# Moving twelve column groups of a modulation product from the conformer stage into the front of the mixer stage

## The chip, the cores and the metric

The kernel runs on one core of a Trainium2 chip. The metric is the device time of one execution in microseconds; the time of the kernel before is the median of three runs. One further execution was profiled, and all rows below come from it.

## The reference, cut to what matters

All work is in float32 on 512 tokens of width 1024. Two attention layers come first (not touched by the change), then two layers of a second kind. Layer 0 mixes with a recurrence and long convolutions, layer 1 with a convolution module (the conformer); each is followed by a mixture of 16 experts. Every layer takes six modulation vectors from a small product of a conditioning vector with a large matrix:

```python
def _adaln(cvec, w_mod, b_mod, n_chunks):
    m = silu(cvec) @ w_mod[:, :n_chunks * D_MODEL] + b_mod[:n_chunks * D_MODEL]
    return [m[:, None, j * D_MODEL:(j + 1) * D_MODEL] for j in range(n_chunks)]

for l in range(2):
    sh1, sc1, g1, sh2, sc2, g2 = _adaln(c, w_mod[l], b_mod[l], 6)
    hl = modulate(rmsnorm(xl, norm1_g[l]), sh1, sc1)
    yl = even_mixer(hl) if l == 0 else conformer(hl)
    xl = xl + g1 * yl
    xl = xl + g2 * moe(modulate(rmsnorm(xl, norm2_g[l]), sh2, sc2))
xl = rmsnorm(xl, final_g)

def even_mixer(h):
    proj = h @ w_in                        # 1024 -> 2560 columns, ten groups of 256
    ...                                    # recurrence (RG-LRU), two FFT convolutions (Hyena)
    return concat([y_a, z]) @ w_out        # 1024 -> 1024
```

The change concerns `sh2, sc2, g2` of layer 1, that is `silu(c) @ w_mod[1][:, 3072:6144]`: a 1024 x 3072 matrix of 12.6 MB. Nothing reads them before the second mixture of experts.

## The kernel before, in words

The program is one long list per engine, made by a scheduler that keeps the order of the source where priorities say nothing else. The stages of the second block follow each other: `even_norm` and the ten projection groups of `even_mixer`, then `hyena` (FFT convolutions, with the out-projection among them), the routing, `moe(0)`, `conformer`, `moe(1)` and the last norm.

**The weight ring.** `wload` (L119 to L139) brings weights in tiles of 512 KB, two to a projection group, by DMAs that SyncE issues in order (L134). The tiles lie in a pool with the tag `ring`; `RE = (3, 3)` gives the mixer three such tiles and three pairs of split tiles, the conformer has rings (6, 4). `split` (L141 to L156) makes of each half tile a rounded copy `wh` on ScalarE (L153) and the rest `wl` on GpSimd (L154), and `mm3` (L158 to L161) multiplies the three pairs that matter. A projection group (`proj_feat`, L368 to L391) is 8 x 2 x 3 = 48 such matmuls of 512 columns, and its last line (L391) calls `fill(1)`.

**The filler.** `fill` (L171) runs one step of a generator `self.filler`, if there is one, and gives its instructions the priority of the place, so that they may stand between the next group's instructions. The generator `adaln` (L195 to L227) makes the modulation vectors: per step it loads two tiles of `w_mod` (1 MB), multiplies them in eight matmuls of 32 x 256 outputs in 32-column strips (L209; each is two records in the profile), and adds the product into `adr` on VectorE (L212 the first time, L214 after that). After the twelfth step, four small matmuls (L219) and one add (L222) put the result into `self.m2[1]`. `cvec` (L178 to L193) loads the conditioning vector and makes its silu. The conformer sets up this filler for column groups 12 to 23 (L1590 and L1591); its eight projection groups call `fill(1)` once by L391 and, from the fourth on, once more by L1636.

**The mixer.** `even_mixer` (L1326) calls `even_norm` and then ten groups of `w_in_2`, called W0 to W9 below. W0 to W3 feed the recurrence, W4 to W9 the convolutions; with W4 to W9 go the steps of the recurrence `rglru` (L1230 to L1247), whose matmuls write `z`, and the transposes `t` (L1362) of the convolved channels `cv`. The tables of the Fourier transform are loaded by `tables` (L1087, tile `dw`), issued from ScalarE's queue, and stand in ScalarE's list among the casts of L153.

## Time and profile before

| what | us |
|---|---|
| median of three runs (lowest to highest) | 3083.48 (3079.88 to 3089.67) |
| the profiled execution, its own time | 3082.83 |
| its span in the trace | 3080.8 |
| two attention layers | 0 to 1560 |
| norm and the ten groups of the mixer | 1560 to 1721 |
| hyena, out-projection, routing | 1721 to 1845 |
| first mixture of experts | 1845 to 2345 |
| conformer | 2345 to 2570 |
| second mixture of experts, last norm | 2570 to 3080 |

The stage limits are round numbers where the work changes; stages overlap at their edges. TensorE is busy for 90% of the span, and the mean clock granted to it is 0.952 of full speed. In the two mixtures of experts the DMA engines are busy nearly throughout; in the stages that the change touches they are not.

A row of a stretch gives, for each engine, its busy microseconds and in brackets the number of instructions, then the granted clock, the mean share in which the 16 DMA engines were busy, and GB/s. A row of a timeline gives start, length, engine, line, operation, output and inputs, count, and in square brackets the idle time before it and what ended it. A row of a chain gives start, length and what was running.

### The profile page before, as it was taken

What the parts mean: (1) busy time and instruction counts of PE and PEld (TensorE: products, weight loads), DVE (VectorE), ACT (ScalarE), POOL (GpSimd) and SP (SyncE); (2) the same over time, 40 slices, a digit from 0 to 9 for tenths busy, and PEclk for the clock granted to TensorE, in tenths of its full rate; (3) what the DMA queues carried; (4) which work ended last, traced back from release to release, by engine and by line L of the source; (5) the groups of instructions that cost most, each with busy time, mean ns of one, the idle gap of its engine ahead of it and who ended that gap; (6) DMA issues with size and microseconds to landing.
All of it is one profiled execution on the core that took longest, in us unless ns stands there. A gap on an engine that the chain in (4) does not pass through costs nothing.

```text
span 3080.8 us, 36122 instructions
## 1 busy us (share of the span) xinstructions
PE 2760.5 (90%) x14014; PEld 1717.2 (56%) x14014; DVE 1514.0 (49%) x2793; ACT 923.3 (30%) x1651; POOL 815.7 (26%) x689
## 2 busy tenths in 40 slices
PE   6889899999899999999998877998888997998887
PEld 2486567776588666765676764433333665333332
DVE  5886664656625645786356773222124663221222
ACT  3434343443423453434335321101002232110101
POOL 2243233332333334343534660000001431000000
PEclk8999899999899999999999888999999998999999
DMA  9632024222253214421331338999996574999996
GB/s 285 210 124 62 22 87 133 90 73 66 73 164 120 76 54 145 137 89 55 116 97 58 103 116 345 420 421 420 421 420 244 154 271 192 420 420 420 420 421 273
DMA packets 225306, 634.26 MB, mean 206 GB/s; under 512 B 12559, under 2 KB 141591, under 8 KB 175728
## 3 DMA queue, kind: packets, MB, share of 16 engines
q1 hardware_dynamic: 213344, 597.62, 51.7%
q0 software_dynamic: 7312, 25.96, 2.5%
q10 hardware_dynamic: 4480, 8.39, 0.7%
q8 instruction: 110, 1.80, 0.3%
q14 instruction: 60, 0.49, 0.1%
HBM read 612.87 MB, written 19.14 MB: 205 GB/s over the span
## 4 chain that ended last, share of the span: by engine, by line
PE 28%; DMA 19%; DVE 5%; POOL 2%; ACT 2%; issue 1%; SPq 0%; DVEq 0%; ACTq 0%; POOLq 0%
DMA mr<-in_exp_w_dram 10%; PE b L1859 10%; DMA mq<-in_exp_w_dram 8%; PE b L159 4%; PE b L161 4%; PE b L160 3%; PE av L763 1%; PE b L209 1%; PE b L1844 1%; PE q L275 1%; DVE lh L1262 0%; PE s L757 0%; DMA scratch<-sb 0%; PE b L324 0%; DVE f L1473 0%
## 5 line engine op out<-in xcount | busy, mean ns | idle before, releaser
L154 POOL TENSOR_TENSOR wl<-ring,wh 128x512 fp32r<-128x512 f32 x304 | 417.3, 1377 | 676.1 <-ACT wh L153 658.0
L153 ACT CAST wh<-ring 128x512 fp32r<-128x512 f32 x304 | 187.4, 620 | 505.9 <-PE b L161 366.6
L1859 PE MATMUL b<-mr,xs 128*64 128x512 f32 x1216 | 283.7, 617 | 37.2 <-DMA mr<-in_exp_w_dram 28.7
L159 PE MATMUL b<-hh,wh 128*128 128x512 f32 (+1 forms) x800 | 294.9, 369 | 3.0 <-DVE sc L621 3.0
L160 PE MATMUL b<-hh,wl 128*128 128x512 f32 (+1 forms) x800 | 290.6, 363 | 1.3 <-POOL wl L154 1.3
L161 PE MATMUL b<-hl,wh 128*128 128x512 f32 (+1 forms) x800 | 289.4, 363 | 0.1
L1859 PE MATMUL b<-mq,xs 128*64 128x512 f32 x832 | 189.2, 604 | 25.2 <-DMA mq<-in_exp_w_dram 16.8
L1859 PEld LDWEIGHTS b<-mr,xs 128*64 128x64 f32 x1216 | 90.1, 141 | 216.6 <-issue 154.6
L1801 POOL DMA_INDIRECT xg<-scratch,ix x16 | 15.5, 967 | 728.0 <-DVE ix L1795 687.5
L763 PE MATMUL av<-P,kv 128*64 128x512 f32 (+2 forms) x672 | 191.8, 518 | 3.0 <-ACT P L813 1.8
L1859 PE MATMUL b<-mr,sb 128*64 128x512 f32 x704 | 159.4, 597 | 18.5 <-DMA mr<-in_exp_w_dram 18.3
L159 PEld LDWEIGHTS b<-hh,wh 128*128 128x128 f32 x800 | 153.3, 192 | 32.4 <-issue 5.6
L160 PEld LDWEIGHTS b<-hh,wl 128*128 128x128 f32 x800 | 153.2, 192 | 26.9 <-issue 4.3
L161 PEld LDWEIGHTS b<-hl,wh 128*128 128x128 f32 x800 | 152.6, 191 | 25.0 <-issue 4.5
L362 PE MATMUL b<-wh,hh 128*128 128x256 f32 x512 | 148.9, 291 | 2.1 <-DVE kb L1160 1.3
L813 ACT ACTIVATE P<-s 128x512 f32<-128x512 f32 (+2 forms) x224 | 116.7, 551 | 113.8 <-PE s L760 110.0
L363 PE MATMUL b<-wl,hh 128*128 128x256 f32 x512 | 148.3, 290 | 0.3 <-POOL wl L154 0.3
L364 PE MATMUL b<-wh,hl 128*128 128x256 f32 x512 | 147.8, 289 | 0.4 <-DVE hl L345 0.4
L1883 DVE TENSOR_TENSOR yl<-yl,b 128x512 f32<-128x512 f32 x32 | 22.0, 688 | 254.1 <-PE b L1859 254.1
L1859 PEld LDWEIGHTS b<-mq,xs 128*64 128x64 f32 x832 | 60.2, 138 | 146.2 <-issue 101.6
L776 POOL TENSOR_TENSOR acc<-acc,P 128x256 f32<-128x256 f32 (+2 forms) x96 | 99.5, 1039 | 118.2 <-ACT P L813 94.2
L757 PE MATMUL s<-q1l,k 128*128 128x512 f32 (+2 forms) x288 | 113.2, 403 | 2.1 <-DVE sc L802 1.6
(564 smaller groups left out, 5681.4 us busy)
## 6 DMA issues: line engine op xcount, KB each, us to landing
mr<-in_exp_w_dram SPq DMA_DIRECT2D x120, 2048.0 KB
mq<-in_exp_w_dram SPq DMA_DIRECT2D x72, 2048.0 KB
ring<-in_w_mod_dram SPq DMA_DIRECT2D x96, 512.0 KB
ring<-in_w_in_dram SPq DMA_DIRECT2D x96, 512.0 KB
ring<-in_ada_w_dram SPq DMA_DIRECT2D x48, 512.0 KB
ring<-in_w_out_dram SPq DMA_DIRECT2D x32, 512.0 KB
bias<-in_BS_dram POOLq DMA_DIRECT2D x16, 512.0 KB, 3.8
bias<-in_BT_dram POOLq DMA_DIRECT2D x16, 512.0 KB, 4.0
```

The costliest lines, as they stand in the source:

```text
L153: nc.scalar.copy(h, src)
L154: nc.gpsimd.tensor_tensor(l, src, h.bitcast(F32), op=ALU.subtract)
L159: m(out, w[0], x[0], start=start, stop=False, skip_group_check=chk)
L160: m(out, w[1], x[0], start=False, stop=False, skip_group_check=chk)
L161: m(out, w[0], x[1], start=False, stop=stop, skip_group_check=chk)
L362: m(o, hh, wh[:, kk, :], start=(k == 0 and i % 2 == 0), stop=False, skip_group_check=True)
L363: m(o, hh, wl[:, kk, :], start=False, stop=False, skip_group_check=True)
L364: m(o, hl, wh[:, kk, :], start=False, stop=stop, skip_group_check=True)
L757: mm(ps, k1[i][:, kt * 128:kt * 128 + 128], q1[i][:, a:b], start=True, stop=False)
L763: mm(av[64 * i:64 * i + 64, a:b], vf(i, kt), P, start=start, stop=stop)
L813: nc.scalar.activation(p[:, :w], ps[:, :w], AF.Exp)
L1859: mm(ps[hf][64 * e:64 * e + 64, :], lhs(k, e), wt[:, e, k2, hf * 512:hf * 512 + 512], start=k == 0, stop=k == 7)
```

## The change

`even_mixer` now makes `cv2` and the filler for column groups 12 to 23 ahead of `even_norm`, takes two steps at once, one more after each of its ten groups by the old last line of `proj_feat`, and empties what is left after the last group. The conformer no longer does either, and its calls of `fill` have nothing to do.

```diff
@@ even_mixer
                 self.hh, self.hl = [self.chunks(hp, nm, KD, N, F32R) for nm in ("hh", "hl")]
+                z2 = self.cvec(tmp, "cv2")
+                self.filler = self.adaln(z2, A["w_mod"][1], 6 * D, self.v("b_mod1"), self.m2[1], tmp, (12, 24))
+                self.fill(2)
                 self.even_norm(tmp)
...
                     next(lru, None)
+                while self.filler is not None:
+                    self.fill(1)
             ub = [self.chunks(up, f"ub{p}", 4, N, F32R) for p in "hl"]
@@ conformer
-                z2 = self.cvec(tmp, "cv2")
-                self.filler = self.adaln(z2, A["w_mod"][1], 6 * D, self.v("b_mod1"), self.m2[1], tmp, (12, 24))
                 w1 = A["cf_w1"]
...
                     self.proj_feat([(wv, 8)], lambda k, s: (hh[k][:], hl[k][:]), (N,), ev)
-                    if c > 2:
-                        self.fill(1)
```

The steps are called M0 to M11 below. Three places show what the change does to the lists.

SyncE at the loads of the second and third projection group, before: only `w_in` tiles, two to a group.

```order
L134 DMA ring_14063<-in_w_in_dram 128x4x256
L134 DMA ring_14065<-in_w_in_dram 128x4x256
L134 DMA ring_14145<-in_w_in_dram 128x4x256
L134 DMA ring_14147<-in_w_in_dram 128x4x256
L134 DMA ring_14227<-in_w_in_dram 128x4x256
```

The same place after, with what each load waits for: `PE` is TensorE's last reading of the tile's old contents, `Pool` is GpSimd's last subtract from it, `DMAHW` an earlier load.

```order
L134 DMA ring_14036<-in_w_in_dram 128x4x256 [waits DMAHW0_49,Pool_49]
L134 DMA ring_14038<-in_w_in_dram 128x4x256 [waits DMAHW4_49,DMAHW3_49,Pool_49]
L134 DMA ring_14112<-in_w_mod_dram 128x4x256 [waits DMAHW5_49,DMAHW1_49,PE_49]
L134 DMA ring_14114<-in_w_mod_dram 128x4x256 [waits DMAHW2_49,PE_49]
L134 DMA ring_14128<-in_w_in_dram 128x4x256 [waits DMAHW4_49,Pool_49]
L134 DMA ring_14130<-in_w_in_dram 128x4x256 [waits DMAHW7_49,Pool_49]
L134 DMA ring_14208<-in_w_mod_dram 128x4x256 [waits DMAHW5_49,PE_49]
L134 DMA ring_14210<-in_w_mod_dram 128x4x256 [waits DMAHW6_49,PE_49]
```

The loads alternate by twos, and the three buffers of the ring divide accordingly: by the tiles' addresses, from W1 on every `w_in` tile (and the first two of `w_out`) lies in one and the same buffer, and the `w_mod` tiles in the other two.

TensorE from the last matmul of W1 into W2, before (`hh`, `hl` are the two parts of the normed input, `b` the sums of a group):

```order
L161 MATMUL b_13984<-hl_3030_13851,wh_14037 128x512
L159 MATMUL b_14061<-hh_3015_13836,wh_14067 128x512
L160 MATMUL b_14061<-hh_3015_13836,wl_14068 128x512
L161 MATMUL b_14061<-hl_3023_13844,wh_14067 128x512
L159 MATMUL b_14062<-hh_3015_13836,wh_14067 128x512
L160 MATMUL b_14062<-hh_3015_13836,wl_14068 128x512
```

One group's matmuls stand directly behind the other's. The same place after:

```order
L161 MATMUL b_14035<-hl_3030_13851,wh_14088 128x512
L209 MATMUL b_14116<-ring_14112,cv2z_13857 32x256 x2
L159 MATMUL b_14126<-hh_3015_13836,wh_14132 128x512
L209 MATMUL b_14116<-ring_14112,cv2z_13857 32x256
L160 MATMUL b_14126<-hh_3015_13836,wl_14133 128x512
L209 MATMUL b_14116<-ring_14112,cv2z_13857 32x256
L161 MATMUL b_14126<-hl_3023_13844,wh_14132 128x512
L209 MATMUL b_14116<-ring_14114,cv2z_13857 32x256 x4
L159 MATMUL b_14126<-hh_3016_13837,wh_14132 128x512
```

The eight matmuls of M3 stand in runs of 2, 1, 1 and 4 with full-width matmuls between. M4, M5 and M10 stand so too; M0, M2, M7, M8 and M11 are one run of eight; M1 is cut by the norm's matmuls (L324) into runs of 1, 3 and 4; M6 into 7 and 1 by matmuls of the recurrence; M9 into one pair and six singles.

ScalarE ahead of the first two loads of the Fourier tables, before: two casts of `w_out` stand between them and the last cast of `w_in`.

```order
L1385 ACTIVATE uah_2991_13799<-ya_14783 128x512
L153 CAST wh_14918<-ring_14868 128x512
L153 CAST wh_15166<-ring_15164 128x512
L153 CAST wh_15182<-ring_15164 128x512
L1087 DMA dw_14959<-in_dft_dram 128x2x256
L1087 DMA dw_14963<-in_dft_dram 128x2x256
L153 CAST wh_15373<-ring_15371 128x512
```

The same place after:

```order
L1388 ACTIVATE uah_2991_13799<-ya_14932 128x512
L153 CAST wh_15065<-ring_15031 128x512
L153 CAST wh_15081<-ring_15031 128x512
L153 CAST wh_15347<-ring_15345 128x512
L153 CAST wh_15363<-ring_15345 128x512
L153 CAST wh_15554<-ring_15552 128x512
L1087 DMA dw_15140<-in_dft_dram 128x2x256
L1087 DMA dw_15144<-in_dft_dram 128x2x256
```

Now a cast of the second tile of `w_out` (15552) stands ahead of them as well, and that tile shares its buffer with the first (15345).

## Rows read from the trace of the kernel before

**Rows 1.** Three stretches by stage: engines' busy us, granted clock, DMA share, GB/s.

```profile
1560.00:1721.00 161.00, 141.29 (x589) 108.95 (x589) 109.58 (x150) 76.54 (x113) 74.03 (x54) 0.94 0.25 81
1721.00:1845.00 124.00, 94.90 (x518) 84.82 (x518) 91.29 (x96) 33.45 (x61) 81.36 (x43) 0.85 0.32 110
...
2345.00:2570.00 225.00, 211.14 (x957) 138.38 (x958) 137.64 (x258) 71.73 (x116) 81.12 (x62) 0.96 0.54 180
```

**Rows 2.** Four stretches of 10 us in the mixer; the first number column is TensorE's.

```profile
1600.00:1610.00 10.00, 10.00 (x46) 8.29 (x45) 3.43 (x6) 4.25 (x8) 5.29 (x4) 1.00 0.31 104
...
1640.00:1650.00 10.00, 5.26 (x20) 3.34 (x18) 7.31 (x7) 3.17 (x6) 6.94 (x5) 1.00 0.17 52
...
1670.00:1680.00 10.00, 7.52 (x23) 4.93 (x24) 6.24 (x9) 7.86 (x12) 1.13 (x1) 0.66 0.00 0
...
1690.00:1700.00 10.00, 6.86 (x24) 4.36 (x23) 8.11 (x14) 6.17 (x9) 3.79 (x3) 0.83 0.10 33
```

**Rows 3.** TensorE's waits, 1560 to 1700: us in total, times, longest.

```profile
PE t L1362 <- DVE cv L1216: 8.0, 2, 4.9
PE b L324 <- DVE nwy L310: 5.3, 1, 5.3
PE z L1230 <- ACT ltr L1233: 4.9, 1, 4.9
```

**Rows 4.** The chain of work that ended last, 1700 to 1760, at the table loads.

```profile
1718.82 0.44 ACT wh L153
1719.29 4.11 DMA dw<-in_dft_dram
```

**Rows 5.** The conformer's L209 alone, as one stretch.

```profile
2370.00:2503.00 133.00, 30.12 (x192) 9.79 (x192) 1.00 0.55 167
```

**Rows 6.** TensorE's timeline in the conformer, at singles, a run of eight, pairs.

```profile
2384.12 0.62 PE L209 MATMUL b<-ring,cv2z 128*32 128x256 f32 x2
...
2385.10 0.62 PE L209 MATMUL b<-ring,cv2z 128*32 128x256 f32 x2
...
2427.90 1.09 PE L209 MATMUL b<-ring,cv2z 128*32 128x256 f32 x16
...
2429.34 1.05 PE L209 MATMUL b<-ring,cv2z 128*32 128x256 f32 x4
...
2430.76 1.05 PE L209 MATMUL b<-ring,cv2z 128*32 128x256 f32 x4
```

**Rows 7.** The same chain, 2490 to 2520, at the conformer's last projection.

```profile
2495.28 0.23 PE b L160
...
2495.78 0.70 ACT cth L1598
...
2503.27 0.34 DVE adr L214
2503.66 0.63 PE b L219 x4
```

**Rows 8.** VectorE's and TensorE's timeline at the conformer's first convolution taps.

```profile
2386.73 0.42 DVE L212 COPY adr<-b 128x256 f32<-128x256 f32 x1 [0.46 <-PE b L209]
...
2387.64 9.29 DVE L1619 SCALAR_TENSOR_TENSOR cu<-cg,vec,cu 128x448 f32<-128x448 f32 x14
...
2397.08 1.09 PE L1624 MATMUL b<-cu,one 128*128 128x512 f32 x2
```

**Rows 9.** The page's groups of the splits: busy us, mean ns, idle before.

```profile
L154 POOL TENSOR_TENSOR wl<-ring,wh 128x512 fp32r<-128x512 f32 x304 | 417.3, 1377 | 676.1 <-ACT wh L153 658.0
L153 ACT CAST wh<-ring 128x512 fp32r<-128x512 f32 x304 | 187.4, 620 | 505.9 <-PE b L161 366.6
```

**Rows 10.** SyncE's timeline at the loads of W3, from the first issue.

```profile
1598.77 11.24 SPq L134 DMA_DIRECT2D ring<-in_w_in_dram  x3
```

**Rows 11.** Busy tenths of the DMA engines, 1596 to 1612, 40 slices of 0.4 us.

```profile
DMA  6000000001389940000000027998000000001679
```

**Rows 12.** TensorE's timeline at two matmuls of the recurrence.

```profile
1650.14 1.94 PE L1230 MATMUL z<-xa,wrec 128*128 128x512 f32 x2 [4.88 <-ACT ltr L1233]
```

## The prediction

> **What bounds the kernel now.** I read the stretches by stage first [rows 1]. In the mixer (1560 to 1721) TensorE is busy for 141.3 of 161 us, in hyena (1721 to 1845) for 94.9 of 124, in the conformer for 211.1 of 225; DMA engines are busy for 0.25 to 0.54. None of the three stages is bound by traffic, so the 12.6 MB are free to be moved; what counts is TensorE and whoever hands it weights.
>
> Inside the mixer the 10 us stretches [rows 2] show two halves. Up to about 1640 TensorE is full (10.00 of 10). After that it has holes (5.26, 7.52, 6.86), and the table of waits [rows 3] says what ends them: the convolved channel `cv` (8.0 us in two waits) and the recurrence's `ltr` (4.9). 12.9 us are thus empty behind a chain of VectorE and ScalarE; 5.3 more are empty in the norm. That is the cover which the change can use. The chain into hyena [rows 4] then runs over a cast of L153 at 1718.82 and the `dw` load behind it at 1719.29, 4.11 us long: the Fourier tables are late, and they stand in ScalarE's list behind casts.
>
> In the conformer TensorE is full from 2370 on, and 30.1 us of it are L209 [rows 5]. At its end the chain [rows 7] goes from the last matmul into `cth` at 2495.78 and on.
>
> **What the conformer gives back.** 192 records of L209 are 96 matmuls. The timeline [rows 6] shows their price from start to start. A mm3 matmul takes 0.23 us [rows 7]. A single L209 with a mm3 beside it has a period of 0.98 (2384.12 to 2385.10), so it costs 0.75; a pair has 1.42 (2429.34 to 2430.76), so 1.19; a whole step of eight in one run takes 1.09. A step thus costs 1.1 us in one run and three to five when cut up; over the stage the busy sum is 30.1, and since TensorE has no hole there, nearly all of it is on the path.
>
> One part is not. The first channel's taps on VectorE start at 2387.64 and take 9.29 [rows 8], to 2396.93, and L1624 reads them at 2397.08. TensorE arrives there just in time now. One step of the filler stands ahead of it, as eight singles, 8 x 0.75 = 6.0 less the 0.15 of slack: about 5.5 us of the gain end in a wait for VectorE. At the end of the stage `adr` L214 (0.34) and L219 (0.63) leave the chain [rows 7], of which I count 0.7, and the small vector instructions of `cvec` are beside other work. Gain: 30.1 - 5.5 + 0.7 = 25.3; adding start-to-start distances in place of busy lengths I get some 2 us more, so I take **26**. Its bounds are 22 (VectorE holds up a second channel as well) and 31 (the early step costs nothing).
>
> By the Trainium skill's page "TensorEngine Tiling (Array Packing)", section Overview, work of 32 columns can be up to four times as fast when tiles are used side by side, so that every step would cost what one in a single run does. By that the stage would give back 12 x 1.09 = 13 us, not 30; its section Tiling Modes adds that a change of mode drains the engine, and the 0.75 of a single in rows 6 agrees with the second sentence, not with the first.
>
> **What the mixer pays.** Five terms.
>
> *The start: +4.* The norm's first product on VectorE now stands behind L212, and so behind M0: 1.09 + 0.42 (L212 [rows 8]) + one single of M1 at 0.75 = 2.3. The other two runs of M1, 3 and 4 long, come ahead of W0: between 0.75 and 1.09 each, 1.5 to 2. The 5.3 us wait in the norm [rows 3] covers none of M0 for certain, since both wait for the same early VectorE work; if it covers all, the term is 0.
>
> *W1 to W4: +16.* Two limits meet. TensorE needs 48 x 0.23 = 11.0 for a group, and its step another 1.1 (M2) or, in runs of 2, 1, 1 and 4, about 4 x 0.75 = 3.0 (M3 to M5): 14.0. The second limit is new. All `w_in` tiles now share one buffer of the ring, so a half can only be loaded when GpSimd has finished the half before it. Such a loop is: issue to landing 3.3 us (1598.77 [rows 10] to the fall of the burst at 1602.0 [rows 11]), a cast of 0.62, two subtracts of 1.3 (the groups' means are 0.62 and 1.38 [rows 9]; undisturbed ones are 1.3), with signals between them some 6.9 us, or 13.8 a group. Each alone gives about 14; walked against each other, with only three pairs of split tiles for the loop to run ahead in, I get 14.3. So 4 x (14.3 - 11.0) = 13.2, 0.9 for the loop's start in W1, and 1.9 for two recurrence matmuls [rows 12] that the new order puts into W2.
>
> *W5 to W9: +4.* M6, M7 and M8 (about 1.8, 1.1 and 1.1) stand in front of the waits for `cv` and lie in holes. M9, as a pair and six singles, costs at least 7 x 0.75 = 5.3, by my walk 6.8 with the router's small matmuls beside it, and M10 3.0; 1.9 come back from W2, and of the rest the holes take about half.
>
> *The Fourier tables: +7.* Before, `dw` goes out at 1719.3, 2 us ahead of the end of W9. After, three casts of `w_out` stand ahead of it in ScalarE's list, the third from a tile whose load waits for the whole first tile to be split. From the last subtract of W9: load 3.3, cast 0.6, subtracts 2.6, load 3.3, cast 0.6 = 10.4 and signals. I get `dw` 5.5 us behind the end of W9: 7.4 later than its neighbours.
>
> *Given back: -2.* Eighteen matmuls of the out-projection, 18 x 0.23 = 4.1, move into that wait; hyena is a chain over other engines, so I count half.
>
> The sum is 4 + 16 + 4 + 7 - 2 = **+29**, say 30 with M11. Bounds: 13 (twelve runs of 1.09 and nothing else) and 43 (the slow rival below).
>
> What stands behind the conformer, up to the end, waits for its data and moves with it; so does the first mixture of experts behind hyena. Net 30 - 26 = +4 on the profiled execution's own 3082.83 (2.0 above its span; 0.65 under the median): **3087 us**.
>
> **Rivals.**
>
> *Faster: the ring doesn't bind and the tables hide.* If casts run far enough ahead, W1 to W4 pay TensorE's share, 1.1 + 3 x 3.0 = 10 in place of 16, the holes take all of W5 to W9, and the out-projection fills the tables' wait (7 - 4 = 3): 4 + 10 + 0 + 3 - 2 = 15, less 26 = -11, 3072 us. For it: 12.9 us of holes [rows 3]. Against it: the loop of 13.8 is made of measured pieces, and its order can't be changed by the engines.
>
> *Slower: the shared buffer's loads meet the `w_mod` loads.* A group now moves four tiles in place of two. The burst of a tile keeps the DMA engines at 8 to 9 tenths [rows 11], so a `w_mod` tile in flight at the same time stretches the landing, at worst by a burst's own 2 us or so; I take 1.4. Each 0.1 us counts twice a group over W1 to W4 and twice more at `w_out`, so ten times: +14, 3101 us. It makes the kernel slower by over 0.3% from a landing of 3.9 us on in place of 3.3 (ten times 0.6 above 3087). For it: `w_mod` loads are issued when TensorE ends a step, at the start of a group, beside the second half's load. Against it: in a group of 14 us the four bursts of 2.4 fill only ten.
>
> *The conformer doesn't give it back.* If VectorE holds up every channel, the gain is 22: 3091 us. In the first channels it is busy for over 9 us in ten; later much less, so I count it little.
>
> *The clock.* In the mixer's holes the granted clock falls to 0.66 and 0.83 of 2.4 GHz [rows 2]: in 0.66 two thirds of 10 us ran at 1.2 GHz. Were the steps to keep it up, the matmuls behind the holes would be 2 to 5 us shorter: 3082 to 3085 us, which changes no verdict. The Trainium skill, page "TensorE: Matmul & The Clock Gate", Part 1, says that the low clock is the default and that activity releases it; whether these steps are activity enough, no row here shows.
>
> **How the numbers follow.** 0.3%, about what a measurement here can tell from no change, is 9.2 us, 3074 to 3093. The forecast, with the clock and the conformer's rival inside it, has 0.47: 3077 to 3093. The faster rival has 0.21, the slower one 0.32, since the mixer's new waits are chained and hold every later stage. The likeliest is 3087. The range has to hold both rivals' centres and leave a tenth at either side: 3070 to 3102.
>
> **What would show it.** L209 in 1558 to 1750 in runs of eight or 2, 1, 1, 4; W4 ending about 20 us later than before, W9 about 24 (1721 before); GpSimd's subtracts in W1 to W4 in pairs 6.9 us apart from half to half, ended by casts, those by loads; `dw` at about 1751; the first mixture of experts about 30 later, the second about 4. In the conformer TensorE waits once, 5 us, for `cu` at L1624. The prediction is wrong if the loads of `w_in` turn out to be issued ahead of the splits, if VectorE or ScalarE ends most waits in W1 to W4, or if the first mixture of experts moves by less than 15 or more than 43.

## The result, and the profile after

The changed kernel takes 3110.89 us (median of 4 runs, 3107.19 to 3113.22) beside 3083.08 us (4 runs, 3079.88 to 3089.67) for the kernel before: a ratio of 1.0092, interval 1.008 to 1.0104. That is 27.8 us slower, on the far side of the rival called slower and outside the range that ended at 3102. The profiled executions differ by as much: their spans are 3107.1 and 3080.8 us.

| | before | after |
|---|---|---|
| median, us | 3083.08 | 3110.89 |
| span of the profiled execution, us | 3080.8 | 3107.1 |
| mean granted clock of TensorE | 0.952 | 0.948 |

Where it went is found by following the same instruction through both traces. The stages ahead of the mixer are untouched by the change, and yet the execution of after arrives 3.63 us earlier there (the L317 matmuls at 1555.95 in place of 1559.58), so 3.63 is added to every later difference. Over the sixteen traces of this study that entry lies between 1553.2 and 1562.1, with nothing changed ahead of it but the place of one 8 KB load (in x_cvfirst); a shift of a few us there is no work of an edit that I could trace. "Step" is the difference from the row above, and is what a term of the prediction stands for.

| the same instruction | before | after | later by | step | predicted |
|---|---|---|---|---|---|
| first product of W0 (L160) | 1571.17 | 1575.36 | 7.8 | start +7.8 | +4 |
| last product of W4 (L161) | 1626.18 | 1648.30 | 25.8 | W1 to W4 +17.9 | +16 |
| last product of W9 (L161) | 1721.06 | 1751.55 | 34.1 | W5 to W9 +8.4 | +4 |
| first `dw` issue | 1718.83 | 1756.98 | 41.8 | tables +7.7 | +7 |
| first product with the tables (L161) | 1725.81 | 1766.93 | 44.8 | landing +3.0 | none |
| first mixture of experts (L1695) | 1865.45 | 1906.42 | 44.6 | hyena -0.2 | -2 |
| conformer's first product (L160) | 2369.14 | 2410.47 | 45.0 | +0.4 | 0 |
| last `cth` of the conformer | 2495.78 | 2518.05 | 25.9 | conformer -19.1 | -26, with the tail |
| L324 behind the conformer's norm | 2510.47 | 2536.03 | 29.2 | tail +3.3 | (in the -26) |
| second mixture of experts (L1768) | 2590.62 | 2616.27 | 29.3 | +0.1 | 0 |
| end of the last stage | 3057.25 | 3083.34 | 29.7 | +0.4 | 0 |

So the mixer and hyena pay 45 us where 29 were forecast, and the conformer with its tail gives back 15.7 where 26 were. 29.7 - 3.63 = 26.1 us, and the spans differ by 26.3. Each such row is read from one execution: the kernel x_both below, with the same code in the mixer, stands 49.1 us late at the conformer in place of 45.0, so a sum over the mixer is good to some 4 us.

**The start.** The next two fences are ScalarE's and VectorE's timelines of the kernel after at the mixer's entry (start, length, engine, line, operation, and in brackets the idle time before it with what ended it).

```profile
1565.28 0.22 ACT L184 ACTIVATE cv2t<-cv 128x16 f32<-128x16 f32 x1 [10.49 <-DMA cv<-in_cv_dram]
```

```profile
1565.73 0.17 DVE L188 TENSOR_SCALAR cv2z<-cv2t 128x16 f32<-128x16 f32 x1
1568.06 0.42 DVE L212 COPY adr<-b 128x256 f32<-128x256 f32 x1 [2.15 <-PE b L209]
1570.79 2.06 DVE L343 SCALAR_TENSOR_TENSOR mt<-xn,s1l,b 128x512 f32<-128x512 f32 x3 [2.31 <-PE b L324]
```

`cv` is 8 KB. SyncE's list of after says when it went out:

```profile
1553.59 1.49 SPq L134 DMA_DIRECT2D ring<-in_w_mod_dram  x3
1555.12 0.49 SPq L1340 DMA_DIRECT2D wrec<-in_lru_w_dram  x1
1555.72 0.38 SPq L182 DMA_DIRECT2D cv<-in_cv_dram  x1
```

Issued at 1555.72 behind three `w_mod` tiles and `wrec` (and `vec`, 172 KB, just ahead of these rows; 2.8 MB together), it is read at 1565.28: 9.6 us for 8 KB. The vector step that makes `cv2z` follows at 1565.73; until then M0 can't run, and behind M0 stand L212 and the norm's first L343. The longest of TensorE's waits, 1560 to 1700, after (us in total, times, longest), is that gap, which no event explains there ("issue"); compare [rows 3].

```profile
PE b L209 <- issue: 8.1, 1, 8.1
```

**W1 to W4.** SyncE's list of after at the loads of `w_in`; each row with x2 spans the two halves of a group.

```profile
1600.89 7.20 SPq L134 DMA_DIRECT2D ring<-in_w_in_dram  x2
...
1616.67 7.30 SPq L134 DMA_DIRECT2D ring<-in_w_in_dram  x2
...
1630.48 7.40 SPq L134 DMA_DIRECT2D ring<-in_w_in_dram  x2
...
1644.31 7.21 SPq L134 DMA_DIRECT2D ring<-in_w_in_dram  x2
```

1630.48 - 1616.67 = 13.8 and 1644.31 - 1630.48 = 13.8: the loop of the shared buffer, at the price that the prediction gave it. The two turns before took 15.8 (from 1600.89) and 18.9 (from an issue at 1582.00). In the longer one a cast waits for TensorE and not for a load, as ScalarE's timeline of after shows (a cast needs one of the three pairs of split tiles, which TensorE still reads); in the other, four instructions of the recurrence stand between two casts, 1611.94 to 1614.66.

```profile
1598.87 0.62 ACT L153 CAST wh<-ring 128x512 fp32r<-128x512 f32 x1 [5.70 <-PE b L161]
```

GpSimd's list of after shows the other end of it: the pair of subtracts 1627.91 to 1630.45, and 0.03 later the next issue.

```profile
1627.91 2.54 POOL L154 TENSOR_TENSOR wl<-ring,wh 128x512 fp32r<-128x512 f32 x2 [4.34 <-ACT wh L153]
```

The stretches of 10 us in the mixer of after (columns as in [rows 2]):

```profile
1560.00:1570.00 10.00, 3.99 (x24) 2.35 (x25) 1.36 (x5) 0.22 (x1) 0.00 (x0) 0.50 0.48 177
...
1640.00:1650.00 10.00, 10.00 (x54) 7.57 (x53) 2.64 (x4) 2.81 (x5) 3.95 (x4) 1.00 0.52 174
1670.00:1680.00 10.00, 5.48 (x18) 3.72 (x19) 7.36 (x12) 7.47 (x11) 0.95 (x1) 0.66 0.48 159
```

The stretch of W4's end is full; the hole of W5 to W9 is still there, at the same 0.66; and the start now stands at 0.50, which is 1.2 GHz for the whole stretch.

**The tables.** The chain of work that ended last, after, ahead of the `dw` load (start, length, what):

```profile
1746.77 3.22 DMA ring<-in_w_out_dram
...
1750.09 0.63 ACT wh L153
...
1750.79 2.54 POOL wl L154 x2
...
1753.34 3.52 DMA ring<-in_w_out_dram
```

This is the forecast chain, load, cast, subtracts, load (and a cast at 1756.96), and `dw` goes out right behind it, 5.4 us after the end of W9 (forecast: 5.5). What was not forecast stands in ScalarE's timeline of after: the load, issued at 1756.98, is cast at 1764.48, 7.5 us later. Before, the same load was cast 3.9 us after its issue (1718.83 to 1722.71), and the one behind it took 4.1 [rows 4].

```profile
1756.98 1.51 ACTq L1087 DMA_DIRECT2D dw<-in_dft_dram  x2
1764.48 0.62 ACT L1089 CAST dfth<-dw 128x512 fp32r<-128x512 f32 x1 [6.89 <-DMA dw<-in_dft_dram]
```

**The conformer.** Its matmuls do end 24.2 us sooner against the stage's start, near the price (30.1 - 5.5 = 24.6), but the stage's end doesn't follow them. ScalarE's timeline of the kernel before, at the last two channels:

```profile
2479.84 0.69 ACT L1598 ACTIVATE cth<-b,chb 128x512 f32<-128x512 f32 x1 [2.13 <-PE b L161]
...
2494.22 0.63 ACT L290 ACTIVATE sq<-cu 128x512 f32<-128x512 f32 x1 [3.36 <-POOL cu L1628]
...
2495.78 0.69 ACT L1598 ACTIVATE cth<-b,chb 128x512 f32<-128x512 f32 x1 [0.41 <-PE b L161]
```

Each of these two `cth` is released by TensorE. One of the seven rounds from `cth` to `cth` before ended otherwise: the third (15.6 us) ends right behind the square `sq` of the channel before, 0.75 us after TensorE was done (2427.97).

```profile
2428.18 0.63 ACT L290 ACTIVATE sq<-cu 128x512 f32<-128x512 f32 x1 [2.31 <-POOL cu L1628]
2428.72 0.67 ACT L1598 ACTIVATE cth<-b,chb 128x512 f32<-128x512 f32 x1
```

The same last two channels after:

```profile
2504.47 0.63 ACT L290 ACTIVATE sq<-cu 128x512 f32<-128x512 f32 x1 [4.79 <-POOL cu L1631]
2505.01 0.67 ACT L1601 ACTIVATE cth<-b,chb 128x512 f32<-128x512 f32 x1
...
2517.51 0.63 ACT L290 ACTIVATE sq<-cu 128x512 f32<-128x512 f32 x1 [6.68 <-POOL cu L1631]
2518.05 0.67 ACT L1601 ACTIVATE cth<-b,chb 128x512 f32<-128x512 f32 x1
```

Now `cth` has no wait of its own: it stands in ScalarE's list right behind `sq`, and `sq` waits for GpSimd. Between the two `cth`, VectorE and GpSimd of after:

```profile
2505.71 0.43 DVE L1602 TENSOR_SCALAR cth<-cth 128x512 f32<-128x512 f32 x1 [2.65 <-ACT cth L1601]
2506.24 0.75 DVE L1604 SCALAR_TENSOR_TENSOR cg<-b,vec,cth 128x512 f32<-128x512 f32 x1
2507.03 0.86 DVE L1607 TENSOR_SCALAR cu<-cg,vec 128x512 f32<-128x512 f32 x1
2507.93 8.20 DVE L1622 SCALAR_TENSOR_TENSOR cu<-cg,vec,cu 128x448 f32<-128x448 f32 x14
```

```profile
2516.22 1.26 POOL L1631 TENSOR_TENSOR cu<-cu,piv 128x512 f32<-128x512 f32 x1 [5.54 <-DVE cu L1622]
```

That closes a loop: `cth`, three vector steps, fourteen taps, a subtraction, `sq`, next `cth`, 13.04 us long (2505.01 to 2518.05). Behind the last channel the tail is slower too. The chain of after there:

```profile
2526.94 3.15 PE q L275 x4
2530.09 3.52 PE b L317 x16
```

One stretch of 4 us at L317, first after, then (next fence) before:

```profile
2530.00:2534.00 4.00, 3.60 (x17) 3.49 (x16) 1.35 (x5) 0.00 (x0) 0.00 (x0) 0.50 1.01 426
```

```profile
2506.00:2510.00 4.00, 2.04 (x17) 1.86 (x16) 2.70 (x15) 0.00 (x0) 0.00 (x0) 1.00 1.05 391
```

The sixteen matmuls of L317, with the tail of one that stands ahead of them, take 3.60 us at a granted clock of 0.50 and 2.04 at 1.00. With the L275 in front of them that is 2.9 of the 3.3 us which the tail loses. Before, M11's matmuls stood a little ahead, and TensorE's longest wait behind the last projection was 1.5 us; after, it waits 3.6 and 2.9. The Trainium skill says of this (page "TensorE: Matmul & The Clock Gate", Part 1) that the low clock is the default and that activity releases it; the rows show the two levels. That the moved matmuls are the cause they don't show, and two of the experiments below speak against it. In x_both M11 still stands there, with the same 1.5 us as TensorE's longest wait, and L317 runs at 0.50; in x_neither_delay no step stands there, and it runs at 1.00:

```profile
2552.00:2556.00 4.00, 3.88 (x17) 3.49 (x16) 1.14 (x5) 0.00 (x0) 0.00 (x0) 0.50 1.00 401
```

```profile
2485.00:2489.00 4.00, 2.14 (x17) 1.86 (x16) 2.67 (x14) 0.00 (x0) 0.00 (x0) 1.00 1.00 422
```

So the 2.9 us can come or stay away with either list, and what decides it stays open.

### The profile page after: what moved, and what is told of

Its sections match the earlier page's. It is cut to its first block, busy times and chain, and to the rows that moved or that the text cites. A ratio compares the mean times of both kernels' runs of the same rounds, so it can differ in the third digit from the quotient of the medians.

```text
span 3107.1 us, 36117 instructions
## 1 busy us (share of the span) xinstructions
PE 2761.2 (89%) x14014; PEld 1715.0 (55%) x14014; DVE 1513.7 (49%) x2793; ACT 920.3 (30%) x1651; POOL 821.6 (26%) x689
## 4 chain that ended last, share of the span: by engine, by line
PE 26%; DMA 20%; DVE 5%; POOL 3%; issue 2%; ACT 2%; SPq 0%; DVEq 0%; ACTq 0%; POOLq 0%
DMA mr<-in_exp_w_dram 11%; PE b L1860 10%; DMA mq<-in_exp_w_dram 7%; PE b L159 3%; PE b L161 3%; PE b L160 3%; POOL wl L154 2%; PE av L763 1%; DMA ring<-in_w_in_dram 1%; PE b L1845 1%; PE q L275 1%; PE s L757 1%; ACT wh L153 0%; DMA scratch<-sb 0%; DVE cu L1622 0%
## 5 line engine op out<-in xcount | busy, mean ns | idle before, releaser
L154 POOL TENSOR_TENSOR wl<-ring,wh 128x512 fp32r<-128x512 f32 x304 | 424.5, 1402 | 708.4 <-ACT wh L153 692.9
L160 PE MATMUL b<-hh,wl 128*128 128x512 f32 (+1 forms) x800 | 291.6, 365 | 2.5 <-POOL wl L154 2.5
L161 PE MATMUL b<-hl,wh 128*128 128x512 f32 (+1 forms) x800 | 290.9, 365 | 0.0
L1860 PE MATMUL b<-mq,xs 128*64 128x512 f32 x832 | 187.7, 600 | 27.4 <-DMA mq<-in_exp_w_dram 20.3
L1802 POOL DMA_INDIRECT xg<-scratch,ix x16 | 15.5, 967 | 728.4 <-DVE ix L1796 687.7
L159 PEld LDWEIGHTS b<-hh,wh 128*128 128x128 f32 x800 | 153.4, 192 | 42.1 <-issue 10.1
L160 PEld LDWEIGHTS b<-hh,wl 128*128 128x128 f32 x800 | 153.2, 191 | 30.0 <-POOL wl L154 5.1
L161 PEld LDWEIGHTS b<-hl,wh 128*128 128x128 f32 x800 | 152.8, 191 | 26.3 <-issue 6.4
```

The source lines that it names most:

```text
L154: nc.gpsimd.tensor_tensor(l, src, h.bitcast(F32), op=ALU.subtract)
L159: m(out, w[0], x[0], start=start, stop=False, skip_group_check=chk)
L160: m(out, w[1], x[0], start=False, stop=False, skip_group_check=chk)
L161: m(out, w[0], x[1], start=False, stop=stop, skip_group_check=chk)
L1860: mm(ps[hf][64 * e:64 * e + 64, :], lhs(k, e), wt[:, e, k2, hf * 512:hf * 512 + 512], start=k == 0, stop=k == 7)
```

## The experiments

Each kernel ran beside the kernel before on the same chip; differences are of medians, against the before of that run.

| kernel | median, us | before, us | ratio | interval |
|---|---|---|---|---|
| x_neither | 3064.93 | 3082.45 | 0.9947 | 0.993 to 0.9964 |
| x_both | 3129.86 | 3082.45 | 1.0157 | 1.014 to 1.0174 |
| x_own | 3125.83 | 3082.45 | 1.0144 | 1.0127 to 1.0161 |
| x_late | 3123.75 | 3082.45 | 1.013 | 1.0112 to 1.0148 |
| x_cvfirst | 3107.95 | 3081.01 | 1.0092 | 1.0075 to 1.0109 |
| x_ring1 | 3105.3 | 3081.01 | 1.0083 | 1.0066 to 1.01 |
| x_contig | 3070.57 | 3081.01 | 0.9964 | 0.9949 to 0.9978 |
| x_neither_delay | 3060.68 | 3081.01 | 0.9939 | 0.9921 to 0.9958 |
| x_neither_slow | 3077.54 | 3081.79 | 0.9987 | 0.9975 to 0.9998 |
| x_before_slow | 3088.18 | 3081.79 | 1.0017 | 1.0007 to 1.0027 |
| x_neither_sq | 3065.06 | 3081.79 | 0.9932 | 0.9914 to 0.995 |
| x_contig_sq | 3073.48 | 3081.79 | 0.9964 | 0.995 to 0.9978 |
| x_after_contig | 3115.32 | 3082.01 | 1.0112 | 1.0095 to 1.0129 |
| x_contig_early | 3070.32 | 3082.01 | 0.9959 | 0.9944 to 0.9973 |

In the four kernels whose name begins with x_neither the second half of the modulation vectors is left out: it is a constant.

### The two halves of the change, each alone

**x_neither**: the filler taken from the conformer and put nowhere. Theory: the conformer gives back 16, and that is all it can. Rival: it gives back 26 as priced, and something else is lost.

```diff
-                z2 = self.cvec(tmp, "cv2")
-                self.filler = self.adaln(z2, A["w_mod"][1], ...
-                self.fill(2)
+                nc.vector.memset(self.m2[1][:, 24:48, :], 0.1)
                 self.even_norm(tmp)
```

> Neither stage makes the second half of the last modulation vectors; the half is filled with a constant, so that part of the computation is left out. This is the conformer's gain alone. Theory A (from the trace after: with the twelve steps gone, a channel of the conformer is paced by a loop of its tanh, VectorE's taps, GpSimd's subtraction and ScalarE's square, about 13.0 us, not by TensorE's 11.0): the conformer gives back 16 us, 3067 us. Theory B (the prediction's: TensorE is the limit in all channels but the first): 26 us, 3057 us.

Measured: 17.5 us under before; in the trace the second mixture of experts stands 15.9 earlier against the mixer's entry, 19.4 being gained at the last `cth` and some 4 lost in the tail, which ran at 0.50 here too. The conformer's gain is 16, not 26, with the mixer as it was.

**x_both**: the filler's code added to the mixer, and the conformer left as it was (so that it makes the vectors a second time).

> The twelve steps stand in the mixer and again in the conformer, where they overwrite the same values: the mixer's cost alone. Theory A (start 8, W1 to W4 18, W5 to W9 4, tables 15): 45 us above before, 3128 us, and the conformer's stretch as before. Theory B (the prediction's 30): 3113 us.

Measured: 47.4 us over before. The mixer's price is 45 to 49 by the traces of after and x_both (in the second the tail's low clock adds 2.4 more), and 47.4 - 17.5 = 29.9 is near what the whole change costs (27.8): the two halves add up to some 2 us.

### The start of the mixer

**x_late** sets the filler up behind the norm.

```diff
+                self.even_norm(tmp)
                 z2 = self.cvec(tmp, "cv2")
                 ...
                 self.fill(2)
-                self.even_norm(tmp)
```

> As the changed kernel, but the conditioning vector's load and the first two steps stand behind the norm in the source and not ahead of it. Theory A (the norm waits for the chain load of cv, tanh, two VectorE instructions, M0 and L212): the norm starts 5 us earlier, 3106 us. Theory C (the two steps cost their matmuls wherever they stand): 3111 us.

Measured: 41.3 us over before, so worse by some 13 than the change itself, where a gain was expected. The trace shows half of the theory right: the norm's L343 starts at 1561.09, 9.4 us sooner than after against the entry. But TensorE's timeline of x_late has this:

```profile
1577.36 2.79 PE L209 MATMUL b<-ring,cv2z 128*32 128x256 f32 x24 [14.78 <-DVE cv2z L188]
```

`cv2z`'s small vector steps now stand behind the norm's work in VectorE's list, TensorE waits 14.8 us for them, and W0 starts 12.0 later than after. The same gate, with its name on it this time: M0 waits for `cv2z`, and who stands behind M0 waits too.

**x_cvfirst** leaves the order and loads `cv` ahead of the ring's tiles.

```diff
+            self.z2 = self.cvec(sp, "cv2")
             with self.rings(*self.RE):
                 self.even_mixer()
...
-                z2 = self.cvec(tmp, "cv2")
+                z2 = self.z2
```

> As the changed kernel, but the conditioning vector is loaded (and its silu made) from the top of the second block, so that its 8 KB load stands ahead of the three w_mod tiles and the recurrence's weights on SyncE's queue and not behind them. Theory A (the norm's first product waits on VectorE behind L212, M0 and so behind that small load, which waits for 2.8 MB): the norm starts 4 to 5 us earlier, 3106 us. Theory C (M0's own tiles are as late): 3111 us, as the changed kernel.

Measured: 3107.95, 26.9 over its before. ScalarE's timeline of x_cvfirst shows the load's wait gone:

```profile
1554.29 0.22 ACT L184 ACTIVATE cv2t<-cv 128x16 f32<-128x16 f32 x1 [0.96 <-DMA cv<-in_cv_dram]
```

The load goes out at 1552.08 and is read 2.2 us later. L343 starts 5.1 us sooner than after, of which 2.8 are left at the first mixture of experts and 1.9 at the end of the last stage. The small load behind the large ones is shown as the cause of the start's late norm; that it is worth something in the whole time isn't: its ratio is 1.0092, that of the change itself.

### The shared buffer

**x_ring1** is the kernel before with one buffer for the ring's tiles instead of three, and no steps in the mixer at all.

```diff
-    RE = (3, 3)
+    RE = (1, 3)
```

> The kernel before, steps in the conformer, but the mixer's ring has one tile in place of three: every w_in and w_out tile lies in one buffer, without any w_mod work beside it. Theory A (the shared buffer's loop of 13.8 us a group against TensorE's 11.0): W1 to W4 are 11 us later, the tables some 7 to 10, by the end 15 to 25 us: 3103 us. Theory C (the changed kernel is slow in the mixer for its extra matmuls alone): under 3 us, 3085 us.

Measured: 24.3 us over before. SyncE's list of x_ring1 at two issues of `w_in`, a whole group (two halves) apart:

```profile
1598.35 0.37 SPq L134 DMA_DIRECT2D ring<-in_w_in_dram  x1
...
1612.15 0.37 SPq L134 DMA_DIRECT2D ring<-in_w_in_dram  x1
```

13.8 us a group, the period of after, with no step on TensorE. This trace's entry into the mixer is 6.4 us before that of the kernel before; counted from there, the end of W4 is 10.1 us late, that of W9 17.4, the first mixture of experts 20.7. W0's first product came 1.4 early by the same count, so the ring by itself gives 11.5 of W1 to W4's 17.9 and 7.3 of W5 to W9's 8.4, or 22 with hyena. (Here all tiles of `w_out` go through the one buffer too; in after only the first two do.)

**x_own** gives the `w_mod` tiles buffers of their own (three of 128 KB each, so that a step is eight loads in place of two), so that `w_in` keeps its three.

```diff
-                w = self.wload(kview(wsrc[...]), 8, 256)
+                w = self.wload(kview(wsrc[...]), 8, 256, **own)
...
+                ... (12, 24), dict(tag="modr", bufs=3, size=256))
```

> As the changed kernel, but the w_mod tiles have a ring of their own (three tiles of 128 KB), so that w_in and w_out tiles go round in all three buffers of the old ring again. Theory A (the shared buffer costs the slips in W1 and W2 and the late Fourier tables; in the steady part TensorE is nearly as long as the loop): 6 us less by the end of W4 and about 10 less at the tables, 3095 us, between 3091 and 3105. Theory C (only TensorE's extra matmuls cost): 3111 us, as the changed kernel.

Measured: 43.4 over before, some 16 slower than the change. TensorE's waits of x_own, 1560 to 1700:

```profile
PE b L209 <- DMA modr<-in_w_mod_dram: 5.0, 3, 2.2
```

It replaced one limit by another: the steps wait for the small tiles. A run with full-sized buffers of their own wasn't made, and this one decides nothing.

**x_after_contig** asks whether it is TensorE or the ring that sets 13.8. In it the steps in the mixer run as one piece each, which takes TensorE's share down (see x_contig).

```diff
     def fill(self, n):
-        with self.background():
+        with self.background() if not self.inline else nullcontext():
...
                 z2 = self.cvec(tmp, "cv2")
+                self.inline = True
```

> The changed kernel with every step's eight matmuls in one run in the mixer. Theory A (in W1 to W4 the shared buffer's loop of 13.8 us sets the group, TensorE's 14.0 only by the side; M9 and M10 cost TensorE time where it is on the path): W1 to W4 gain next to nothing, 1 to 3 us, W5 to W9 some 3, together 5 us under the changed kernel, 3106 us. Theory B (TensorE's cut-up steps are the cost): 2 us for each of M3, M4, M5 and M10 and 5 for M9, 13 us under it, 3098 us.

Measured: 33.3 over before, no better than after. The stretches of x_after_contig in W3 and W4:

```profile
1620.00:1630.00 10.00, 9.00 (x38) 6.79 (x38) 3.64 (x7) 2.40 (x4) 3.69 (x3) 1.00 0.56 180
1630.00:1640.00 10.00, 9.15 (x51) 6.48 (x50) 3.77 (x7) 4.18 (x8) 3.44 (x3) 1.00 0.47 155
```

and its SyncE list:

```profile
1628.02 7.36 SPq L135 DMA_DIRECT2D ring<-in_w_in_dram  x2
...
1641.84 0.37 SPq L135 DMA_DIRECT2D ring<-in_w_in_dram  x1
```

TensorE has room (9.00 and 9.15 of 10 at full clock) and this turn still takes 13.8. So in W4 the buffer's loop is the limit, and cheaper steps help little: W4 ends 22.7 us late against the entry, in place of 25.8, the 1 to 3 us that theory A gave. The total says nothing more of the steps, since the recurrence's matmuls came out in another order as well, and in W5 TensorE waits 5.4 us for one of their inputs (`lti`); 8.2 us are lost there.

### Why the conformer gave back 16

Theory: with the steps gone the loop over `cth`, VectorE, GpSimd and `sq` (13.0 us a channel) takes over from TensorE (11.1 for a channel's 48 matmuls). Rival: TensorE is still what paces, or a load.

**x_neither_slow** and **x_before_slow** add three vector instructions to each channel, between `cth` and `cg`, to x_neither and to the kernel before.

```diff
                         nc.vector.tensor_scalar(th[:], th[:], 1.0, 0.5, op0=ALU.add, op1=ALU.mult)
+                        for _ in range(3):
+                            nc.vector.tensor_scalar(th[:], th[:], 1.0, 0.0, op0=ALU.mult, op1=ALU.add)
```

> As the kernel in which neither stage makes the modulation half (a constant stands there), with three needless VectorE instructions more per channel of the conformer, behind the tanh's, 0.43 us each. Theory A (without the steps a channel is a loop over ScalarE, VectorE and GpSimd): the 1.3 us a channel are paid in nearly all eight, 10 us above the kernel without them, 3075 us. Theory B (TensorE sets the channel): under 3 us, 3067 us.

> The kernel before with the same three VectorE instructions more per channel of the conformer. Theory A (with the steps TensorE's 14 us a channel hide the loop's 13): 0 to 4 us above before (the last channel pays its 1.3 in any case), 3085 us. Theory C (VectorE is on the path there too): 10 us, 3093 us.

Measured: 3077.54, 12.6 over x_neither's 3064.93; and 3088.18, 6.4 over its before (5.2 by the ratio; in the trace 3.3 at the last `cth` and the rest in the tail). Without the filler a channel goes from 13.6 to 15.5 us and the kernel pays for it, as ScalarE's timeline of x_neither_slow shows (15.48 between the two `cth`):

```profile
2440.17 0.63 ACT L290 ACTIVATE sq<-cu 128x512 f32<-128x512 f32 x1 [11.58 <-POOL cu L1631]
2440.70 0.67 ACT L1599 ACTIVATE cth<-b,chb 128x512 f32<-128x512 f32 x1
...
2455.38 0.63 ACT L290 ACTIVATE sq<-cu 128x512 f32<-128x512 f32 x1 [1.33 <-POOL cu L1631]
2456.18 0.69 ACT L1599 ACTIVATE cth<-b,chb 128x512 f32<-128x512 f32 x1 [0.17 <-PE b L161]
```

With the filler it goes from 16.2 to 16.7. The rival fails on the first pair. The second shows that the loop was close behind already, closer than I had expected: in x_before_slow five of the last six `cth` come 0.35 to 3.0 us after TensorE was done, behind `sq`, where before it was one.

**x_neither_delay** was meant to open the loop: `sq` of a channel written behind the next channel's `cth`.

```diff
-                        for i in ((0, 1) if c == 1 else (c,) if c else ()):
...
+                        for i in ((0,) if c == 1 else (c - 1,) if 1 < c < 7 else (7,) if c == 7 else ()):
+                            done(i)
```

> As the kernel in which neither stage makes the modulation half (a constant stands there, so that part is left out), and in the conformer the subtraction and the square of a channel are issued one channel later, behind the next channel's tanh on ScalarE. Theory A (tanh of a channel stands behind the square of the one before, so that VectorE's taps and GpSimd are a loop of 13.0 us with it): the loop opens, channels take TensorE's 11.0 to 11.5, 3056 us. Theory C (VectorE or GpSimd is full by itself): 3065 us, as without the delay.

Measured: 3060.68, 20.3 under before where x_neither had 17.5, and channels of 13.1 to 13.6 from the third on. The order on ScalarE didn't change, since the scheduler put `sq` ahead of `cth` again, so it says nothing of the loop. Most of what its trace has over that of x_neither is the tail: from the last `cth` to L324 it takes 15.1 us in place of 18.5, at the full clock shown above.

**x_neither_sq** opens it in another way: the squares go to GpSimd.

```diff
-                                s(i, u[i][:])
+                                s(i, u[i][:], nc.gpsimd if i < 7 else None)
```

> As the kernel in which neither stage makes the modulation half (a constant stands there), but the squares of the conformer's first seven channels are made on GpSimd, not on ScalarE, so that ScalarE's list has nothing between one tanh and the next that waits for VectorE's taps. Theory A (ScalarE's order closes the loop): a channel falls from 13.0 to TensorE's 11.0 or so, 7 us less than with the squares on ScalarE, 3058 us. Theory C (GpSimd's own list, with the splits of the weights behind the subtraction, closes it as well): 3065 us, no change.

Measured: 3065.06, no different from x_neither. But ScalarE's timeline of x_neither_sq shows the loop open and, in its place, one hole:

```profile
2444.40 0.62 ACT L153 CAST wh<-ring 128x512 fp32r<-128x512 f32 x1 [11.67 <-issue]
...
2452.73 0.69 ACT L1599 ACTIVATE cth<-b,chb 128x512 f32<-128x512 f32 x1 [2.13 <-PE b L161]
...
2463.88 0.69 ACT L1599 ACTIVATE cth<-b,chb 128x512 f32<-128x512 f32 x1 [2.13 <-PE b L161]
```

11.15 us from `cth` to `cth`, TensorE's own pace, both released by TensorE; four of the seven rounds are so. So the loop is what held a channel at 13. The gain is eaten by the 11.67 us wait ahead of the cast at 2444.40, in a round of 21.2. As far as the trace tells, it is a cast of the output projection's weights, whose load goes out only at 2439.46, behind GpSimd's last split from that buffer; and that split stands in GpSimd's list behind a subtraction that waited 4.2 us for VectorE, and behind the moved square. That is the other theory's cause, in one round.

### A better version

If a step costs 1.09 in one run and 3 to 5 cut up [rows 6], it need not be moved to become cheap.

**x_contig** is the kernel before with the same edit to `fill` as in x_after_contig, and `self.inline = True` ahead of the conformer's loop.

> The kernel before, but each step of the filler keeps its place in the order, so that its eight matmuls stand in one run between two groups in place of alternating with the group's matmuls. Theory A (a run costs 1.1 us in place of 2.5, and then the 13.0 us loop of ScalarE, VectorE and GpSimd sets the channel): 8 us less, 3075 us. Theory B (TensorE alone sets the channel): 16 us less, 3067 us. Theory C (runs and single ones cost the same): 3083 us.

Measured: 3070.57, 10.4 us under before, and so 38 under the change (10.4 + 27.8). The same 192 records, alone, in x_contig; compare [rows 5]:

```profile
2360.00:2510.00 150.00, 13.26 (x192) 5.94 (x192) 0.92 0.64 202
```

13.26 us where 30.12 were. The channels come at 14.5 on average in place of 16.2.

**x_contig_sq** adds the squares on GpSimd, **x_contig_early** puts two steps ahead of the conformer's norm (and one at c = 3 and c = 5 each).

> The kernel before with every step in one run (as tried before) and the squares of the first seven channels on GpSimd. Theory A: channels take TensorE's 12.4 in place of the loop's 13.0, 4 us less than the runs alone, 3066 us. Theory C: 3070 us, no change.

> The kernel before with every step in one run, and two of the twelve already ahead of the conformer's norm, where TensorE waits for VectorE; the later channels take one less. Theory A: the two hide in that wait if their tiles have landed, and channels 4 to 7 lose a step each where the loop is near: 2 us under the runs alone, 3069 us. Theory C (the norm waits behind the steps on TensorE, as it did in the mixer): 4 us above them, 3075 us.

Measured: 3073.48 (0.9964 of its before) and 3070.32 (0.9959): neither differs from x_contig. In x_contig TensorE is done 0.6 to 6.4 us ahead of each of the last six `cth`, so the loop paces it with the steps in one piece. In x_contig_sq TensorE is done right ahead of six of the eight, and the total is the same; what paces those channels was not followed. The theory that the first steps' place matters can't be told from the one that it doesn't.

## Why the prediction was wrong

The forecast was "same", at +4. No single term failed alone: the mixer's five came to 45 in place of 29, and the conformer's one to 15.7 in place of 26. By its own steps:

- **W1 to W4, +16: held** (17.9). The loop of 13.8 was put together from a landing, a cast and two subtracts of [rows 9 to 11], and it runs at 13.8 in after, x_ring1 and x_after_contig. ([rows 10] calls its loads those of W3; by their count they are W4's, which changes no sum.) "Each alone gives about 14" was right, and the loop is the firmer limit of the two: with TensorE's share made smaller a turn still takes 13.8 (x_after_contig). That the total fits is in part luck: the groups took 17.8, 16.3, 14.0 and 13.9 us, not four times 14.3 and 2.8 besides. The first two are longer by what the turns showed: a wait of 5.7 us for a pair of split tiles, a coupling that the prediction named ("only three pairs of split tiles") and priced at a few tenths, and the recurrence's work on ScalarE, of which it counted the matmuls alone.
- **The Fourier tables, +7: held** in the issue (7.7, `dw` 5.4 behind W9), and missed in the landing: 7.5 us instead of the 4.1 of [rows 4], 3 more. The load goes out among three late `w_out` tiles and the loads of `K`; that these slow it is likely, and no run tested it. The step "load 3.3, cast 0.6 ..." priced the way to the issue and took the landing over unchanged.
- **The start, +4: failed, +7.8.** "Both wait for the same early VectorE work" was said of M0 and the norm. M0 waited for something else, the 8 KB `cv` load behind 2.8 MB on SyncE's queue. The prediction listed the loads that the ring moves and never walked `cvec`'s one past that queue; x_cvfirst shows that it was the wait.
- **W5 to W9, +4: mis-sized, +8.4.** It counted steps and holes and left the ring out: x_ring1 pays 7.3 there without any step. After 1640 the loop still hands out the tiles of `w_in`.
- **Given back, -2: failed, about 0.** What took it is not known.
- **The conformer, -26: failed, -15.7.** This is the largest miss of a single term. "Since TensorE has no hole there, nearly all of it is on the path" reads a full engine as the only limit. A second limit lay 3 us a channel below (13.0 without the steps, against 16.2), and with the steps it had set one of the seven rounds already. It could have been added up beforehand from the trace of before, where [rows 7 and 8] hold two of its pieces: `cth` 0.7, three vector steps of 2.0, taps of 8.2 to 9.3, a subtraction of 1.3, a square of 0.6. That the square stands ahead of the next `cth` needs ScalarE's list; the Trainium skill (page "Perfetto Trace Analysis", section "Tensor Engine Instruction (MATMUL, LD_WEIGHTS)") calls ScalarE, VectorE and GpSimd strictly first in, first out, and the `cth` rows with no idle time behind `sq` agree. The loop takes 5.1 us of TensorE's 24.2 at the last `cth`, and the tail takes another 3.3, of which 2.9 are the 1.2 GHz that x_both has with the steps in place. The 5.5 set aside for the first channel came as 3.3.
- **The rivals.** "The conformer doesn't give it back" had the right mechanism ("if VectorE holds up every channel") and the wrong price, 22: it took VectorE alone and not the ring of four engines, and it was "counted little". The "slower" rival had the right sign and the wrong cause for the ring: the steady loop takes 13.8 us with `w_mod` loads beside it (after) and without any (x_ring1), and the two `w_out` loads of the chain land in 3.22 and 3.52. Only `dw` landed later. "The clock" didn't come: the hole's stretch is at 0.66 as before.

Against the +4 of the forecast the end moved by 29.7: 16 of that gap are in the mixer and hyena, 10 in the conformer. The prediction said it would be wrong if the first mixture of experts moved by more than 43; it moved by 44.6.

**What stays open.** Of the 45 us, some 22 are the ring's (x_ring1, if one buffer for all tiles weighs what the division in after does) and 8 the start's. The other 15 are not split between the steps' matmuls, the low clock at the start, and the later loads: x_own, which should have shown the mixer with steps and without the shared buffer, was no clean test. Why the tail behind the conformer runs at one clock or the other is open too.

## What to carry to other kernels

When an engine that is busy all the time is relieved, add up the next limit before counting the relief: follow one round of the stage through every engine, with each engine's own order, and take the longest loop. Work that is moved takes its loads with it: count which buffers they now share, which turns a prefetch into a loop of load, cast and release, and which small load ends up behind large ones in a queue. And before moving cheap work that costs much because it is cut up, try leaving it in one piece where it is (x_contig gained 10 us so; in the mixer the same edit gained nothing, so each place is measured by itself).

## What the runs showed of the hardware

- An 8 KB load issued behind 2.8 MB on the same queue was read 9.6 us after its issue; issued ahead of the `w_mod` tiles and `wrec`, it was read after 2.2 us (x_cvfirst).
- The same 192 records of 32-column matmuls had 30.12 us of busy time cut into singles and pairs among full-width ones, and 13.26 left in one piece per step: 0.157 and 0.069 us a record. The drain at a change of mode, which the prediction quoted from the Trainium skill (page "TensorEngine Tiling (Array Packing)", Tiling Modes) and gave no price, agrees with that difference; no run here separates it from other costs of the mixed order.
- The same sixteen small matmuls took 3.58 us at a granted clock of 0.50 and 1.95 at 1.00. With the same list in front of them and the same waits to a tenth of a us they ran at 1.00 in one execution (before) and at 0.50 in another (x_both).
